# Moving recombination, PSUM order and a buffer's DMA queue around step 8 of an fp32 attention layer on one core

## The chip, the cores and the metric

The kernel runs on one core of one Trainium2 chip. The metric is device time in microseconds of one execution. The engines are TensorE (PE; its weight loads are PEld), VectorE (DVE), ScalarE (ACT), GpSimd (POOL) and SyncE (SP, which only issues DMAs here). GpSimd can issue DMAs too; its transfers go through another queue than SP's (q0 and q1 in the page's table of queues). Each engine runs its instructions in the order in which they stand in the program, and a waiting instruction holds up all behind it on that engine.

## What is computed

One layer of an encoder trunk on 512 tokens (8 rows by 64 columns) of width 2048, in float32:

```python
h = rms_norm(x, norm_pre)
q, k, v, z = split(h @ w_in, 4)                 # w_in: 2048 x 8192
o = neighbourhood_attention(q, k, v, rpb)       # 16 heads of 128, window 8 x 16, bias, softmax
y = (o * silu(z)) @ w_out                       # w_out: 2048 x 2048
x = x + rms_norm(y, norm_post)
```

## The kernel before

Every matmul is made of three: an operand is split into hi (a cast to the fp32r type, on ScalarE, line 287) and lo (source minus hi, on VectorE, line 288), and hi·hi, lo·hi and hi·lo are added up in PSUM. Splits of the stationary operand are `split_a` (lines 159, 160).

The work is a list of 512 slots `m`, each one tile of 128 by 512 of the weights. Step 0 and step 8 (`PLAIN`) multiply plainly: 32 slots each, 16 per half `n`, twelve matmuls of 512 columns per slot into four PSUM tiles `u8_n_0` to `u8_n_3` (`mm_plain`). The other steps (1 to 7 for the projections of two heads each, 9 for the last part of the output) use seven products of sums of blocks, 56 slots, in three PSUM chains X, Y and Z (`mm_seven`, `combine`); the quarters of the result come out of additions on VectorE. The last product of step 7 ends in chain Z (`u7Z0`, `u7Z1`), and `combine` takes it out with four instructions (lines 418, 419): s minus u, e minus u, for each of two. Only then can step 8's tiles `u8_0_2` and `u8_0_3` begin, because they lie in the same PSUM buffers (tags u2, u3).

The loop runs `prep(m + 2)` (loads' tile, hi, lo), then the matmuls of slot m, then what a table `beside` has at m (`at`). In that table stand the attention of heads 14 and 15 (`turn`, `split_k`, `split_q`, `scores`, ..., `split_p`, `pv`, `gated`), which runs between the slots of step 8, and the loads that follow. A scheduler turns this into the orders of the engines: the order of the code is its priority, and instructions issued through the wrappers `sync`, `dve` and `act` stay in the order of the code among themselves; others may move.

Names that matter below:

- `raw`: 4 buffers for weights just loaded (SP, lines 254 and 261). A load waits until the instruction that reads the buffer's former tile is done. raw424 to raw455 are step 8's slots 0 to 31; raw512 and on are the tiles for the sums.
- `zw`: 2 buffers. `load_z(k)` loads a block of w_out (line 133), `prep(512 + k)` adds raw(512 + k) to it on VectorE (line 269), `keep_z(k)` stores the sum to the DRAM tile `wsum` (line 136), which step 9 reads back. `sum_prep` says in which slot this is done. The next load into the buffer waits for the store. For k = 6 and 7 zw is loaded once more, with other blocks.
- `graw`: the gated heads in DRAM, written and fetched through GpSimd's queue (lines 608, 618). The buffers t0 to t7 and the pairs gr8 to gr12 take them as step 8's stationary operand (a0_0, a0_1 and so on: tile of slot k, part).
- `k14l`, `q14l`, `pt15_1l`: lo parts of attention operands of heads 14 and 15, made on VectorE, read by TensorE's score (line 525) and output (line 596) matmuls. `zm15` is head 15's gated output (line 602), whose split is a7_2, the stationary operand of slot 15.
- `WARM`: matmuls on a tile of ones at the start (line 97), before any data is there.

Of the kernel before, what the change touches and what calls it, by code (L numbers as in the profile page):

```python
# [10 lines left out]
F32 = mybir.dt.float32  # L11
F32R = mybir.dt.float32r
AF = mybir.ActivationFunctionType
ALU = mybir.AluOpType
# [11 lines left out]
SCALE = HD ** -0.5  # L26
NEG = -1.0e30
TBL = 48
WARM = 8
SHIFT = P // 2  # L30


# [9 lines left out]
NSTEP = HEADS // 2  # L42
NPASS = 7
KH = KT // 2
SLOTS = NPASS * KH
FIRST = 2 * KT
PLAIN = (0, NSTEP)
SPAN = [FIRST if step in PLAIN else SLOTS for step in range(NSTEP + 2)]
LAST = NSTEP + 1
A11, S1, A12, N2, A22, N4, N3 = range(NPASS)  # L50
B11, B12, B21, B22 = range(4)
# [17 lines left out]
def na_block(ctx: ExitStack, tc: tile.TileContext, xT, x, gpre, gpost, w, rpb, out):  # L69
    nc = tc.nc  # L70
    sync, dve, act = (InOrder(tc, e) for e in (nc.sync, nc.vector, nc.scalar))
# [23 lines left out]
    warm = px.tile([P, P], F32, tag="T", name="warm")  # L95
    for i in range(WARM):
        nc.tensor.matmul(warm, ones, ones, start=True, stop=True)
# [30 lines left out]
    Z = {}  # L128
    wsum = dp.tile([KH, P, L], F32, name="wsum")

    def load_z(k):
        Z[k] = cp.tile([P, L], F32, tag="zw", name=f"zw{k}", bufs=2)
        nc.sync.dma_start(Z[k], w[LAST, B12, k])

    def keep_z(k):
        nc.sync.dma_start(wsum[k], Z.pop(k))


    X = {}
# [72 lines left out]
    def base(step):  # L212
        return sum(SPAN[:step])

    def where(m):

        step = 0
        while m >= SPAN[step]:
            m -= SPAN[step]
            step += 1  # L220
        p, k = divmod(m, KT if step in PLAIN else KH)
        return step, LATE[p] if step == LAST else p, k

    def is_raw(m):
        step, p, _ = where(m)
        return step in PLAIN or p not in ((0, 1, 6) if step == LAST else (0, 6))
# [6 lines left out]
    def sum_prep(m):  # L233

        m -= base(NSTEP)
        at_m = {6 + 2 * k: [k] for k in range(KH)}
        for k in range(KH):
            at_m.setdefault(22 + 2 * k if k < KH - 2 else 15 + 2 * k, []).append(KH + k)
        return [N + j for j in at_m.get(m, ())]
# [25 lines left out]
    def prep(m):  # L265
        if m >= N:
            i, k = divmod(m - N, KH)
            t = T[k] if i and k < KH - 2 else Z[k]
            nc.vector.tensor_tensor(t, t, raws.pop(m), ALU.add)
            for r in at_prep.get(m, ()):  # L270
                load_raw(r)
            return
        step, p, k = where(m)
        plain = step in PLAIN
        src = raws.pop(m) if is_raw(m) else Z[k] if (step, p) == (LAST, 6) and k >= KH - 2 else T[k]
        if not plain and p in (1, 3, 4) and (step, p) != (LAST, 1):
            nc.vector.tensor_tensor(T[k], T[k], src, ALU.add)  # L277
            src = T[k]
        if m >= N - KH:
            hi, lo = (A(k, o).rearrange("p a b -> p (a b)") for o in (S1, N3))  # L280
        else:
            hi, lo = (wp.tile([P, L], F32R, tag=t, name=f"{t}{m}") for t in ("hi", "lo"))
        W[m] = (hi, lo)
        if step == 0 and p == 0:
            take_x(k, (hi, src))
        if m:
            (act if m < 4 else nc.scalar).copy(hi, src)  # L287
        nc.vector.tensor_tensor(lo, src, hi.bitcast(F32), ALU.subtract)  # L288
        if plain:
            if step == 0 and p == 1 and k >= KH:  # L290
                load_t(1, B11, k - KH)
        elif p == 4 and step < LAST:
            load_t(step, B12, k)
        elif p == 5 and step < LAST:
            nc.vector.tensor_tensor(T[k], T[k], src, ALU.add)  # L295
        elif p == 6 and (step + 1 < NSTEP or step == LAST and k < KH - 2):
            load_t(min(step + 1, LAST), B11, k)
        elif p == 0 and step == LAST:
            nc.sync.dma_start(T[k], wsum[k])
        for r in at_prep.get(m, ()):  # L300
            load_raw(r)
# [4 lines left out]
    def chain(p):  # L306
        return "XYXYZYZ"[p]
# [4 lines left out]
    def mm_plain(m):  # L312
        step, n, k = where(m)
        if k == 0:
            if n == 0:
                U[n] = [pm.tile([P, L], F32, tag=f"u{j}", name=f"u{step}_0_{j}") for j in range(4)]
            else:
                U[n] = [px.tile([P, L], F32, tag="ST"[j // 2], name=f"u{step}_1_{j}") for j in range(4)]
        hi, lo = W.pop(m)
        kk = k % KH  # L320
        a = (A(kk, A11), A(kk, N4)) if k < KH else (A(kk, A12), A(kk, A22))
        ops = [
            (a[j // 2][:, i, j % 2 * P : j % 2 * P + P], w, j, i2)
            for i2, (i, w) in enumerate(((0, hi), (1, hi), (0, lo)))
            for j in range(4)
        ]
        if k == KT - 1:
            ops.sort(key=lambda op: op[2])
        for l, r, j, i in ops:
            nc.tensor.matmul(U[n][j], l, r, start=k == 0 and i == 0, stop=k == KT - 1 and i == 2)  # L330
            if step and k == KT - 1 and i == 2:
                finish(n, j, U[n][j], small(("v", "qk")[n], f"y{n}_{j}"))
# [12 lines left out]
    def mm_seven(m):  # L345
        step, p, k = where(m)
        c = chain(p)
        if begins(step, p) and k == 0:
            b = (step + (c == "Y")) % 2
            if step == LAST and c == "X":  # L350
                U[c] = [px.tile([P, L], F32, tag="T", name=f"u{step}{c}{s}") for s in range(2)]
            else:
                U[c] = [pm.tile([P, L], F32, tag=f"u{2 * b + s}", name=f"u{step}{c}{s}") for s in range(2)]
        if m >= N - KH:

            s, kk = divmod(2 * k, KH)
            for j in (kk, kk + 1):
                products(N - KH + j, (s,))
            if kk + 2 == KH:
                finish(2, s, U["X"][s], C[LAST]["11"][:, s, :])  # L360
                final(s)
        else:
            products(m, (0, 1))
            W.pop(m)
            if k == KH - 1:
                combine(step, p)
# [19 lines left out]
    def combine(step, p):  # L386
        u = U[chain(p)]
        c = C.setdefault(step, {})
        if step == LAST:
            combine_last(c, u, p)  # L390
        elif p == 0:
            c["12"] = pair(f"s1_{step}")
            for s in range(2):
                nc.scalar.copy(c["12"][:, s, :], u[s])
        elif p == 1:
            c["21"] = pair(f"s5_{step}")
            for s in range(2):
                nc.scalar.copy(c["21"][:, s, :], u[s])
        elif p == 2:
            c["11"] = pair(f"c11_{step}")  # L400
            for s in range(2):
                nc.scalar.activation(c["11"][:, s, :], u[s], AF.Copy, scale=rc[:, s : s + 1])
        elif p == 3:
            c["22"] = pair(f"e_{step}")
            for s in range(2):
                nc.vector.tensor_tensor(c["22"][:, s, :], u[s], c["12"][:, s, :], ALU.subtract)
            nc.vector.tensor_tensor(c["21"], c["22"], c["21"], ALU.subtract)
        elif p == 4:
            for s in range(2):
                nc.vector.tensor_tensor(c["22"][:, s, :], u[s], c["22"][:, s, :], ALU.add)  # L410
        elif p == 5:
            for s in range(2):
                nc.vector.tensor_tensor(c["12"][:, s, :], u[s], c["12"][:, s, :], ALU.subtract)
            for s in range(2):
                scale_c(c["12"], s, 0)
        else:
            for s in range(2):
                nc.vector.tensor_tensor(c["21"][:, s, :], u[s], c["21"][:, s, :], ALU.subtract)
                nc.vector.tensor_tensor(c["22"][:, s, :], c["22"][:, s, :], u[s], ALU.subtract)  # L419
            for s in range(2):  # L420
                scale_c(c["21"], s, 2)
            for s in range(2):
                scale_c(c["22"], s, 2)
# [199 lines left out]
    def at(m, f, *args):  # L623
        beside.setdefault(m, []).append(lambda: f(*args))
# [124 lines left out]
        sync.dma_start(xres[t, q], x_v[16 * t : 16 * t + 16, :, q * L : (q + 1) * L])  # L749

    for k in range(KH):
        at(base(NSTEP) + 1 + 2 * k, load_z, k)
        at(base(NSTEP) + 5 + 2 * k, keep_z, k)
    for k in (KH - 2, KH - 1):

# [18 lines left out]
            load_raw(k)  # L774
    nc.scalar.preload_act_table_set("exp_and_others")
    for m in range(-AHEAD, N):
        if m + AHEAD < N - KH:
            prep(m + AHEAD)
            for j in late_prep(m + AHEAD) + sum_prep(m + AHEAD):
                prep(j)  # L780
        if 0 <= m and m + 4 < KT:
            load_x(m + 4)
        if m < 0:
            continue
        (mm_plain if where(m)[0] in PLAIN else mm_seven)(m)
        for f in beside.get(m, ()):
            f()

# [54 lines left out]
```

## Time and profile before

| what | us |
|---|---|
| median of 3 runs | 895.12 (893.77 to 897.36) |
| profiled execution | 893.32 |
| its span, first to last instruction | 891.5 |
| first real matmul starts | 4.92 |
| step 8 begins on TensorE | 702.05 |
| step 9 begins on TensorE | 802.91 |

The page gives for each engine the busy time, its share of the span and the number of instructions. The mean granted clock of TensorE is 0.998. A row of a timeline has the start in us, the duration, engine, line, operation, output<-inputs (buffer numbers left out), shapes and the count; in brackets the idle time before it on its engine and what ended that. Rows of SPq are issues of DMAs. A row of a table of windows has the stretch, its length, then busy us and started instructions of PE, PEld, DVE, ACT and POOL, the granted clock, the mean busy share of the 16 DMA engines and GB/s.

### The profile page before, as it was taken

To read this page: it belongs to the slowest core of one execution; us is meant where nothing else is said; L and a number is where in the kernel's file an instruction comes from. 1 tells how busy PE (TensorE), PEld (TensorE's weight loads), DVE (VectorE), ACT (ScalarE), POOL (GpSimd) and SP (SyncE) were. 2 spreads that over 40 slices of the span, in tenths; PEclk is the share of its full clock that TensorE was granted. 3 is DMA by queue.
4 is the path that set the end of the run, shared out by engine and by line. 5 is a ranking of instruction groups with operands and counts; after the bars stand their busy time and mean duration, and the time that the engine had idled before them with its cause. 6 is when DMAs were issued, how large, how long until landed. Compare 5 with 4: busy or idle time off the path is not lost. (4 is left out here: it accounts for less than half of the span.)

```text
span 891.5 us, 13143 instructions
## 1 busy us (share of the span) xinstructions
PE 876.9 (98%) x4176; PEld 729.5 (82%) x4176; DVE 734.3 (82%) x1370; ACT 559.4 (63%) x1091; POOL 20.9 (2%) x42
## 2 busy tenths in 40 slices
PE   9999999999999999999999999999999999999995
PEld 8888888888888888888888888888888787888874
DVE  5467979897988898889879987998799855896995
ACT  7566857585758575856675667566756755446551
POOL 0000000000000000000000000000010100000000
PEclk9999999999999999999999999999999999999999
DMA  8768357635663676376547653764487566677875
GB/s 274 228 182 255 98 172 234 204 126 181 238 190 112 215 217 188 106 232 217 168 124 234 209 175 119 243 208 154 137 267 224 169 225 213 204 234 228 254 223 170
DMA packets 91734, 174.95 MB, mean 196 GB/s; under 512 B 10512, under 2 KB 10512, under 8 KB 91664
## 3 DMA queue, kind: packets, MB, share of 16 engines
q1 hardware_dynamic: 88992, 166.24, 60.1%
q0 software_dynamic: 2240, 7.34, 2.4%
q8 instruction: 32, 0.52, 0.2%
q10 hardware_dynamic: 432, 0.53, 0.2%
q14 instruction: 38, 0.31, 0.1%
HBM read 164.11 MB, written 9.96 MB: 195 GB/s over the span
## 5 line engine op out<-in xcount | busy, mean ns | idle before, releaser
L287 ACT CAST hi<-t 128x512 fp32r<-128x512 f32 x318 | 196.0, 619 | 127.7 <-DVE lo L288 29.2
L288 DVE TENSOR_TENSOR lo<-t,hi 128x512 fp32r<-128x512 f32 x318 | 217.0, 689 | 38.3 <-ACT hi L287 36.5
L288 DVE TENSOR_TENSOR lo<-raw,hi 128x512 fp32r<-128x512 f32 x184 | 126.1, 689 | 53.3 <-ACT hi L287 40.1
L287 ACT CAST hi<-raw 128x512 fp32r<-128x512 f32 x180 | 111.5, 620 | 90.9 <-DMA raw<-in_w 21.7
L330 PE MATMUL u<-hi,a 128*128 128x512 f32 x512 | 131.7, 394 | 1.2 <-DVE e L419 1.1
L277 DVE TENSOR_TENSOR t<-t,raw 128x512 f32<-128x512 f32 x184 | 123.1, 688 | 3.5 <-DMA raw<-in_w 3.0
L330 PEld LDWEIGHTS u<-hi,a 128*128 128x128 f32 x512 | 95.5, 189 | 21.5 <-DVE e L419 1.7
L330 PE MATMUL u<-lo,a 128*128 128x512 f32 x256 | 70.8, 390 | 0.0
L330 PEld LDWEIGHTS u<-lo,a 128*128 128x128 f32 x256 | 48.1, 188 | 10.1
L295 DVE TENSOR_TENSOR t<-t,raw 128x512 f32<-128x512 f32 x56 | 37.3, 688 | 7.3 <-DMA raw<-in_w 7.3
L377 PE MATMUL u9Y<-hi,a 128*128 128x512 f32 x96 | 26.8, 394 | 1.4 <-ACT hi L287 1.3
L377 PE MATMUL u5Y<-hi,a 128*128 128x512 f32 x96 | 26.9, 397 | 0.0
L377 PE MATMUL u3Y<-hi,a 128*128 128x512 f32 x96 | 26.9, 397 | 0.0
L377 PE MATMUL u4Y<-hi,a 128*128 128x512 f32 x96 | 26.9, 397 | 0.0
L377 PE MATMUL u6Y<-hi,a 128*128 128x512 f32 x96 | 26.9, 397 | 0.0
L377 PE MATMUL u7Y<-hi,a 128*128 128x512 f32 x96 | 26.8, 396 | 0.0
L377 PE MATMUL u1Y<-hi,a 128*128 128x512 f32 x96 | 26.8, 396 | 0.0
L377 PE MATMUL u2Y<-hi,a 128*128 128x512 f32 x96 | 26.8, 396 | 0.0
L377 PEld LDWEIGHTS u9Y<-hi,a 128*128 128x128 f32 x96 | 17.7, 188 | 6.3 <-ACT hi L287 2.3
L608 POOL DMA_DIRECT2D graw<-zm x14 | 7.8, 555 | 561.4 <-DVE zm L602 561.4
L558 ACT ACTIVATE edge<-edge,col 128x192 f32<-128x192 f32 x32 | 14.5, 454 | 8.9 <-DVE col L551 8.9
L377 PEld LDWEIGHTS u4Y<-hi,a 128*128 128x128 f32 x96 | 17.4, 189 | 3.2
(447 smaller groups left out, 1935.0 us busy)
## 6 DMA issues: line engine op xcount, KB each, us to landing
raw<-in_w SPq DMA_DIRECT2D x392, 256.0 KB, 3.0
t<-in_w SPq DMA_DIRECT2D x126, 256.0 KB, 2.9
bm<-in_rpb SPq DMA_DIRECT2D x16, 384.0 KB, 4.5
x<-in_xT SPq DMA_DIRECT2D x16, 256.0 KB, 3.8
graw<-zm POOLq DMA_DIRECT2D x14, 256.0 KB, 3.5
sq<-in_x SPq DMA_DIRECT2D x6, 512.0 KB, 5.3
xres<-in_x SPq DMA_DIRECT2D x12, 256.0 KB, 4.1
zw<-in_w SPq DMA_DIRECT2D x10, 256.0 KB, 2.7
```

The source lines that it names most:

```text
L277: nc.vector.tensor_tensor(T[k], T[k], src, ALU.add)
L287: (act if m < 4 else nc.scalar).copy(hi, src)
L288: nc.vector.tensor_tensor(lo, src, hi.bitcast(F32), ALU.subtract)
L295: nc.vector.tensor_tensor(T[k], T[k], src, ALU.add)
L330: nc.tensor.matmul(U[n][j], l, r, start=k == 0 and i == 0, stop=k == KT - 1 and i == 2)
L377: nc.tensor.matmul(U[c][s], l, r, start=begins(step, p) and k == 0 and n == 0, stop=k == KH - 1 and n == 2, skip_group_check=True,)
L558: nc.scalar.activation(p, p, AF.Exp, bias=nm[:, i : i + 1], accum_out=sm[:, i : i + 1])
L608: nc.gpsimd.dma_start(graw[h], z_of[h])
```

## The change

Five edits: nine warm-up matmuls in place of eight; zw loaded and stored through GpSimd's queue, its loads of k = 2 to 7 two slots later, and each sum for k = 0 to 7 one slot later; the last slot of step 7 put in the program ahead of the prep of two slots on, with the recombination and one lo kept in order; and in step 8's first slot the twelve matmuls listed with the tiles of the free PSUM buffers first (all of tiles 0 and 1, then 2, then 3).

```diff
-WARM = 8
+WARM = 9
...
     def load_z(k):
         Z[k] = cp.tile([P, L], F32, tag="zw", name=f"zw{k}", bufs=2)
-        nc.sync.dma_start(Z[k], w[LAST, B12, k])
+        nc.gpsimd.dma_start(Z[k], w[LAST, B12, k])
 
     def keep_z(k):
-        nc.sync.dma_start(wsum[k], Z.pop(k))
+        nc.gpsimd.dma_start(wsum[k], Z.pop(k))
...
-        at_m = {6 + 2 * k: [k] for k in range(KH)}
+        at_m = {7 + 2 * k: [k] for k in range(KH)}
...
-        nc.vector.tensor_tensor(lo, src, hi.bitcast(F32), ALU.subtract)
+        (dve if m == base(NSTEP) + 1 else nc.vector).tensor_tensor(lo, src, hi.bitcast(F32), ALU.subtract)
...
         if k == KT - 1:
             ops.sort(key=lambda op: op[2])
+        elif step and n == 0 and k == 0:
+            ops.sort(key=lambda op: max(op[2], 1))
...
+            vector = dve if step + 1 == NSTEP else nc.vector
             for s in range(2):
-                nc.vector.tensor_tensor(c["21"][:, s, :], u[s], c["21"][:, s, :], ALU.subtract)
-                nc.vector.tensor_tensor(c["22"][:, s, :], c["22"][:, s, :], u[s], ALU.subtract)
+                vector.tensor_tensor(c["21"][:, s, :], u[s], c["21"][:, s, :], ALU.subtract)
+                vector.tensor_tensor(c["22"][:, s, :], c["22"][:, s, :], u[s], ALU.subtract)
...
-        at(base(NSTEP) + 1 + 2 * k, load_z, k)
+        at(base(NSTEP) + (3 if k > 1 else 1) + 2 * k, load_z, k)
...
     for m in range(-AHEAD, N):
+        if m == base(NSTEP) - 1:
+            mm_seven(m)
         if m + AHEAD < N - KH:
             prep(m + AHEAD)
...
-        (mm_plain if where(m)[0] in PLAIN else mm_seven)(m)
+        if m != base(NSTEP) - 1:
+            (mm_plain if where(m)[0] in PLAIN else mm_seven)(m)
```

What the orders of the engines show of it. VectorE at the end of step 7, before (s5_7 and e_7 are the recombination of the last product, lo425 the split for slot 1, a5_0 and a5_1 splits of a fetched head):

```order
L160 TENSOR_TENSOR a4_1_121<-t4_140,a4_1_121 128x256
L160 TENSOR_TENSOR a5_0_124<-t5_141,a5_0_124 128x256
L288 TENSOR_TENSOR lo425_7443<-raw425_7362,hi425_7442 128x512
L418 TENSOR_TENSOR s5_7_6785<-u7Z0_7094,s5_7_6785 128x512
L419 TENSOR_TENSOR e_7_7070<-e_7_7070,u7Z0_7094 128x512
L418 TENSOR_TENSOR s5_7_6785<-u7Z1_7095,s5_7_6785 128x512
L419 TENSOR_TENSOR e_7_7070<-e_7_7070,u7Z1_7095 128x512
L288 TENSOR_TENSOR lo426_7463<-raw426_7375,hi426_7462 128x512
L160 TENSOR_TENSOR a5_1_125<-t5_141,a5_1_125 128x256
```

And of the change (the lines are those of the changed kernel; the wrapper's is 65):

```order
L161 TENSOR_TENSOR a4_1_122<-t4_141,a4_1_122 128x256
L161 TENSOR_TENSOR a5_0_125<-t5_142,a5_0_125 128x256
L161 TENSOR_TENSOR a5_1_126<-t5_142,a5_1_126 128x256
L65 TENSOR_TENSOR s5_7_6786<-u7Z0_7095,s5_7_6786 128x512
L65 TENSOR_TENSOR e_7_7071<-e_7_7071,u7Z0_7095 128x512
L65 TENSOR_TENSOR s5_7_6786<-u7Z1_7096,s5_7_6786 128x512
L65 TENSOR_TENSOR e_7_7071<-e_7_7071,u7Z1_7096 128x512
L65 TENSOR_TENSOR lo425_7458<-raw425_7363,hi425_7457 128x512
L290 TENSOR_TENSOR lo426_7464<-raw426_7376,hi426_7463 128x512
```

lo425 has gone behind the four instructions, a5_1 has come ahead of them.

VectorE some 7 us later, where the first sum and the operands of head 14's scores are made, before:

```order
L288 TENSOR_TENSOR lo428_7515<-raw428_7429,hi428_7514 128x512
L269 TENSOR_TENSOR zw0_7512<-zw0_7512,raw512_7493 128x512
L288 TENSOR_TENSOR lo429_7576<-raw429_7446,hi429_7575 128x512
L486 TENSOR_TENSOR k14l_7538<-tk14_7532,k14h_7537 128x512
L480 SCALAR_TENSOR_TENSOR q14l_7547<-tq14_7541,q14h_7546 128x512
```

And of the change:

```order
L290 TENSOR_TENSOR lo428_7516<-raw428_7430,hi428_7515 128x512
L290 TENSOR_TENSOR lo429_7577<-raw429_7461,hi429_7576 128x512
L270 TENSOR_TENSOR zw0_7513<-zw0_7513,raw512_7519 128x512
L492 TENSOR_TENSOR k14l_7539<-tk14_7533,k14h_7538 128x512
L486 SCALAR_TENSOR_TENSOR q14l_7548<-tq14_7542,q14h_7547 128x512
```

zw0 stands directly ahead of k14l. On SP its raw512 stands behind raw431 in place of ahead of it. On TensorE the score matmul that reads q14l follows directly on the one that reads k14l, and two more u matmuls (one until now between those two) stand ahead of them.

VectorE at the end of head 15's attention, before:

```order
L288 TENSOR_TENSOR lo438_7929<-raw438_7831,hi438_7928 128x512
L269 TENSOR_TENSOR zw5_7924<-zw5_7924,raw517_7932 128x512
L288 TENSOR_TENSOR lo439_7960<-raw439_7873,hi439_7959 128x512
L486 TENSOR_TENSOR pt15_0l_7955<-pt15_0_7949,pt15_0h_7954 128x512
L288 TENSOR_TENSOR lo440_7992<-raw440_7900,hi440_7991 128x512
L269 TENSOR_TENSOR zw6_7987<-zw6_7987,raw518_7995 128x512
L486 TENSOR_TENSOR pt15_1l_7983<-pt15_1_7977,pt15_1h_7982 128x512
L288 TENSOR_TENSOR lo441_8030<-raw441_7935,hi441_8029 128x512
L602 SCALAR_TENSOR_TENSOR zm15_7812<-o15_8012,zm15_7812 128x512
L160 TENSOR_TENSOR a7_2_134<-zm15_7812,a7_2_134 128x2x256
```

And of the change:

```order
L290 TENSOR_TENSOR lo438_7928<-raw438_7830,hi438_7927 128x512
L290 TENSOR_TENSOR lo439_7956<-raw439_7869,hi439_7955 128x512
L492 TENSOR_TENSOR pt15_0l_7951<-pt15_0_7945,pt15_0h_7950 128x512
L270 TENSOR_TENSOR zw5_7986<-zw5_7986,raw517_7959 128x512
L290 TENSOR_TENSOR lo440_7991<-raw440_7899,hi440_7990 128x512
L492 TENSOR_TENSOR pt15_1l_7982<-pt15_1_7976,pt15_1h_7981 128x512
L290 TENSOR_TENSOR lo441_8026<-raw441_7931,hi441_8025 128x512
L270 TENSOR_TENSOR zw6_8063<-zw6_8063,raw518_8029 128x512
L608 SCALAR_TENSOR_TENSOR zm15_7808<-o15_8008,zm15_7808 128x512
L161 TENSOR_TENSOR a7_2_135<-zm15_7808,a7_2_135 128x2x256
```

zw5 is now behind pt15_0l, and zw6 behind pt15_1l and lo441, directly ahead of zm15.

SP has 18 DMAs fewer and POOL 18 more. On POOL the loads of zw0 and zw1 stand directly behind the set-up of `ident`, ahead of everything else; zw0's store and what follows stand behind the eight fetches of t0 to t7; the two fetches of gr12 stand behind zw3's store.

## The prediction

> **What bounds the kernel now.** I read the page's first part, then who waited for whom on TensorE, then the chain that ended last.
>
> ```profile
> PE 876.9 (98%) x4176; PEld 729.5 (82%) x4176; DVE 734.3 (82%) x1370; ACT 559.4 (63%) x1091; POOL 20.9 (2%) x42
> ```
>
> TensorE is busy in 98% of the span: 14.6 us of 891.5 are left. Its waits, each with its total, count and longest in us:
>
> ```profile
> PE u9Y L377 <- ACT hi L287: 1.3, 1, 1.3
> PE o L596 <- DVE pt_1l L486: 1.1, 1, 1.1
> PE u L330 <- DVE e L419: 1.1, 1, 1.1
> PE warm L97 <- DVE ones L94: 1.1, 1, 1.1
> ```
>
> Only the second and third stand where the change works (step 8, from 702 us). The first is in the end game, the fourth before any data. What remains is mostly the stretch after the last matmul, which nothing here touches. So the edits compete for about 2.2 us, 0.25% of the time. In the chain, step 8 is one unbroken run once its attention is done, and TensorE is what finishes it:
>
> ```profile
> 756.61 46.46 PE u L330 x204
> 803.07 10.88 PE u9Z L377 x48
> ```
>
> That is 0.228 us per matmul (46.46 / 204). A microsecond won or lost by TensorE ahead of 756 us therefore moves everything behind it. In the end game each raw load is issued when the split ahead of it frees a buffer, so those waits move with it too.
>
> **The ninth warm-up matmul.** Timeline of TensorE at the start (start, duration, count at the row's end):
>
> ```profile
> 1.05 3.78 PE L97 MATMUL warm<-ones 128*128 128x128 f32 x16 [1.05 <-DVE ones L94]
> 4.92 2.83 PE L330 MATMUL u<-hi,a 128*128 128x512 f32 x8
> 5.49 1.06 PE L330 MATMUL u<-hi,a 128*128 128x512 f32 x2
> 5.91 0.91 PE L330 MATMUL u<-hi,a 128*128 128x512 f32 x2
> ```
>
> Eight in the code are 16 in the trace, 0.236 us each, ending at 4.83. A ninth adds two, 0.47 us, to 5.30; the first real matmul now starts at 4.92, so it comes 0.38 later. The early real matmuls follow each other at 0.42 us (5.49, 5.91) and not at 0.228, though the granted clock reads 1.00 at the start too (the window row below). So what is displaced runs at half rate: 0.38 / 0.42 is 0.9 of a matmul, made up later at 0.228, **+0.2 us**. If the full rate came later by as much, it would be +0.4; if data are late anyway (next part), 0.
>
> [...]
>
> **The first two zw loads now open POOL's queue.** They wait for nothing, so they go out right after POOL's last set-up instruction, instead of at 32 us:
>
> ```profile
> 1.18 0.29 POOL masks.py:199 TENSOR_SCALAR_AFFINE_SELECT ident<-ident 128x128 f32<-128x128 f32 x1
> 3.00:4.00 1.00, 1.00 (x7) 1.00 (x7) 0.17 (x1) 0.00 (x0) 0.00 (x0) 1.00 1.08 407
> 6.44 0.62 ACT L65 CAST hi<-raw 128x512 fp32r<-128x512 f32 x1
> 8.50 1.98 PE L330 MATMUL u<-hi,a 128*128 128x512 f32 x8
> ```
>
> In the window 3 to 4 the DMA engines are full (share 1.08) at 407 GB/s. Two tiles of 256 KB are 0.52 MB, 1.3 us of that, so the loads that x and raw wait for can come up to 1.3 us later. The cover is ScalarE's lead: the second tile's hi ends at 7.06 and TensorE takes it at 8.50, 1.44 us. I take **0**; with the cover gone it costs up to 1.3.
>
> [...] No row of this trace has both queues full at the start.
>
> **Recombination ahead of lo425.** VectorE up to the first e, the second e, and TensorE's wait:
>
> ```profile
> 702.04 0.76 DVE L160 TENSOR_TENSOR a<-t,a 128x256 fp32r<-128x256 f32 x2
> 702.71 0.69 DVE L288 TENSOR_TENSOR lo<-raw,hi 128x512 fp32r<-128x512 f32 x1
> 703.31 0.69 DVE L418 TENSOR_TENSOR s<-u7Z,s 128x512 f32<-128x512 f32 x1
> 703.91 0.68 DVE L419 TENSOR_TENSOR e<-e,u7Z 128x512 f32<-128x512 f32 x1
> 705.10 0.68 DVE L419 TENSOR_TENSOR e<-e,u7Z 128x512 f32<-128x512 f32 x1
> 704.64 0.74 PE L330 MATMUL u<-hi,a 128*128 128x512 f32 x2 [1.07 <-DVE e L419]
> 705.45 1.12 PE L330 MATMUL u<-hi,a 128*128 128x512 f32 x4
> ```
>
> u8_0_2 waits for the first e (ends 704.59) and u8_0_3 for the second (705.78). The order rows show that lo425 (0.60, from 702.71 to 703.31) leaves the place ahead of s, but a5_1 (half a tile wide, 0.33 by the first row's pair, 702.04 to 702.71) moves in: s starts 0.27 earlier, at 703.04. TensorE then starts u8_0_2 at 704.37 and has that group done by 705.18, one more matmul by 705.41, and waits for the second e until 705.56; it had not waited there. After these matmuls it is about **0.1 us** ahead. Bounds: 0, and 1.1 if the wait went altogether, which VectorE, busy up to s, does not allow. The sorted order of TensorE's first tile changes one row here, since it stood nearly so already.
>
> **zw0 moves behind lo429, onto k14l and q14l.** VectorE, SP's issue and TensorE:
>
> ```profile
> 709.66 0.69 DVE L288 TENSOR_TENSOR lo<-raw,hi 128x512 fp32r<-128x512 f32 x1
> 708.49 0.33 SPq L254 DMA_DIRECT2D raw<-in_w  x1
> 711.16 0.69 DVE L269 TENSOR_TENSOR zw<-zw,raw 128x512 f32<-128x512 f32 x1 [0.81 <-DMA raw<-in_w]
> 714.51 0.28 PE L525 MATMUL s<-k14h,q14l 128*128 128x256 f32 x1
> 755.96 0.33 SPq L254 DMA_DIRECT2D raw<-in_w  x1
> 761.03 0.69 DVE L269 TENSOR_TENSOR zw<-zw,raw 128x512 f32<-128x512 f32 x1 [2.31 <-DMA raw<-in_w]
> ```
>
> raw512 now stands one place later in the ring of four: it needs lo428 done (709.66 + 0.69, some 0.5 earlier by the saved and moved work, 709.9). With its own landing of 2.65 us (708.49 to 711.14) it is there at 712.55. Behind it on VectorE are zw0, k14l and q14l: q14l ends 1.9 us after zw0 starts, at 714.45. TensorE reaches that score matmul at about 714.6 (714.51, less 0.1, plus one u moved ahead of it). So nothing is lost at 2.65, 0.4 at the 3.1 us that is usual, and 2.3 at the 5.05 of the slowest such load (755.96 to 761.01). Value **+0.2**, nearest to its own landing.
>
> **zw6 leaves the place ahead of pt15_1l.** SP's issues, VectorE, TensorE:
>
> ```profile
> 744.81 0.42 SPq L254 DMA_DIRECT2D raw<-in_w  x1
> 745.72 0.69 DVE L288 TENSOR_TENSOR lo<-raw,hi 128x512 fp32r<-128x512 f32 x1 [1.43 <-ACT hi L287]
> 748.84 0.69 DVE L269 TENSOR_TENSOR zw<-zw,raw 128x512 f32<-128x512 f32 x1 [2.43 <-DMA raw<-in_w]
> 750.46 0.38 SPq L254 DMA_DIRECT2D raw<-in_w  x1
> 754.04 0.69 DVE L269 TENSOR_TENSOR zw<-zw,raw 128x512 f32<-128x512 f32 x1 [2.69 <-DMA raw<-in_w]
> 754.65 0.68 DVE L486 TENSOR_TENSOR pt_1l<-pt,pt_1h 128x512 fp32r<-128x512 f32 x1
> 755.39 0.39 PE L596 MATMUL o<-pt_1l,vh 128*128 128x256 f32 x1 [1.15 <-DVE pt_1l L486]
> ```
>
> VectorE sits 2.69 us for raw518 with pt15_1l behind it, and TensorE waits for that. In the new order only zw5 and lo440 are ahead. zw5's raw517 needs lo438 done (746.41) and took 4.0 us (744.81 to 748.82): zw5 at 750.45, lo440 at 751.05, pt15_1l done by 752.35, 1.7 us before TensorE asks (754.08). The whole gap goes: 755.39 to 754.08, **-1.3 us**.
>
> What is late next: zw6 now stands ahead of zm15, the head's last product.
>
> ```profile
> 756.65 0.69 DVE L602 SCALAR_TENSOR_TENSOR zm<-o,zm 128x512 f32<-128x512 f32 x1 [0.72 <-PE o L596]
> 757.37 0.62 ACT L159 CAST a<-zm 128x512 fp32r<-128x512 f32 x1 [3.87 <-DVE zm L602]
> 756.45 2.85 PE L330 MATMUL u<-hi,a 128*128 128x512 f32 x11
> ```
>
> zm15 feeds a7_2, ScalarE casts it by 757.99, and after seven matmuls of hi440 TensorE takes it at 758.04: no slack today. With TensorE 1.3 earlier zm15 is wanted at 755.35. raw518 can go out when lo440 is done (751.75) and took 3.5 us (750.46 to 753.96): zw6 at 755.3, zm15 at 755.9, 0.55 late. Value **+0.5**; 0 if raw518 lands in 2.65, 1.05 if in 4.0.
>
> On POOL gr12's two fetches now stand behind zw3's store. ScalarE's cast of the second, and the matmuls that want it:
>
> ```profile
> 741.25 0.62 ACT L159 CAST a<-gr 128x512 fp32r<-128x512 f32 x1 [1.04 <-DMA gr<-graw]
> 747.54 2.10 PE L330 MATMUL u<-hi,a 128*128 128x512 f32 x8
> ```
>
> The cast ends 5.7 us before TensorE starts on it; zw3's store would have to wait longer than that, so 0. The remaining moves (step 0's splits, step 8 behind zm15, SP's shorter list) fall where TensorE's list above shows no wait of a microsecond: 0, and a few tenths either way if that cover were gone.
>
> **Sum.** +0.2 + 0 - 0.1 + 0.2 - 1.3 + 0.5 = -0.5 us. The profiled execution took 893.32 (span 891.5), so 892.8; it was 1.8 faster than the median of the runs shown, 895.12, and for a median I forecast **894.6 us**.
>
> **The rivals.**
> - *No new wait* (chance 0.25): raw512 and raw518 land in about 2.65 us. Then -1.3 - 0.1 + 0.2 = -1.2, 893.9. For it: raw512 did, on quiet DMA engines. Against it: 3.5 to 5 for the later ones.
> - *Late raw tiles in front of attention* (0.2), which ends slower: the zw sums still sit in VectorE's in-order queue, now ahead of q14l and zm15. With 4.0 us for both, q14l costs 1.3 and zm15 1.05: 0.2 - 0.1 + 1.3 - 1.3 + 1.05 = +1.1, 896.2. It decides from about 3.5 us for both, where the two waits reach 1.2.
> - *Starved start* (0.1): the two early loads delay x and raw by the full 1.3 us, and ScalarE's lead of 1.44 is already spent on the later first cast. +1.3 in place of +0.2: 895.7.
> - *It does not do what it says*: the tiles of PSUM are freed hardly sooner. This is in the forecast already, as 0.1 of a wait of 1.07.
>
> **How the numbers follow.** The forecast has 0.45. The sum's ends are -1.6 (no new wait, no start cost, 0.3 at the recombination) and +1.8 (late raw tiles, and half the starved start). The three runs before spread over 3.6 us, so a median of such runs is uncertain by about 0.5 more: 893.0 to 897.4, from 895.12. About 0.5% is what a measurement of this kernel can tell from no change, 4.5 us: every case above lies within it. I leave 0.03 for faster, which would need more than all of TensorE's waits here, and 0.04 for slower, a stall in a queue that I have not seen: same 0.93.
>
> **What would show it.** Right: TensorE's list has no wait on pt_1l any more; its wait on e is 0.7 to 1.0 us, with a second small one behind it; zw waits of VectorE stand ahead of q14l and zm15, and TensorE waits for q14l or for a7_2 by a few tenths. The warm-up ends at 5.3 and the first real matmul follows at once. Wrong: a wait on x or raw before 20 us; a wait for pt_1l still there; the wait on e gone altogether; an end game that gains or loses a microsecond by itself, since its loads land in 3 to 5 us.

## The result, and the profile after

| | before | changed |
|---|---|---|
| median, us | 895.17 (893.6 to 897.36, 8 runs) | 900.41 (898.31 to 902.67, 8 runs) |
| ratio, 95% interval | | 1.0057 [1.0039, 1.0075] |
| profiled execution (span) | 893.32 (891.5) | 902.52 (900.8) |
| granted clock, mean | 0.998 | 0.994 |

The change makes the kernel 5.2 us slower. The first part of the page of the changed kernel:

```profile
PE 880.9 (98%) x4178; PEld 730.6 (81%) x4178; DVE 733.5 (81%) x1370; ACT 559.8 (62%) x1091; POOL 30.7 (3%) x60
```

TensorE's idle time went from 14.6 to 19.9 us, and its busy time rose by 4.0, though there are only two matmuls more: the trace's busy time counts a matmul longer at the lower clock, and takes in waits too short to be listed (both below). Its waits in the profile of the changed kernel (total, count, longest, in us):

```profile
PE u L335 <- DVE zm L608: 4.2, 1, 4.2
PE u9Y L382 <- DVE s L445: 1.1, 1, 1.1
PE warm L97 <- DVE ones L94: 1.1, 1, 1.1
PE u9Y L382 <- ACT hi L288: 1.0, 1, 1.0
PE tz L479 <- DVE k14l L492: 0.8, 1, 0.8
PE u L335 <- DVE e L65: 0.8, 1, 0.8
...
PE tz L479 <- DVE k9l L492: 0.2, 1, 0.2
```

The wait for pt_1l is gone, as forecast. In its place stands one of 4.2 us for zm, head 15's gated output. The timeline of the changed kernel shows what leads to it: a selection of the rows of SyncE's issues (SPq), VectorE and TensorE, each row with start, duration and, in brackets, the idle time ahead of it.

```profile
750.21 0.69 DVE L290 TENSOR_TENSOR lo<-raw,hi 128x512 fp32r<-128x512 f32 x1 [1.43 <-ACT hi L288]
750.93 0.33 SPq L255 DMA_DIRECT2D raw<-in_w  x1
756.06 0.69 DVE L270 TENSOR_TENSOR zw<-zw,raw 128x512 f32<-128x512 f32 x1 [3.12 <-DMA raw<-in_w]
756.67 0.69 DVE L290 TENSOR_TENSOR lo<-raw,hi 128x512 fp32r<-128x512 f32 x1
757.16 0.42 SPq L65 DMA_DIRECT2D gpost<-in_gpost  x1
757.68 0.38 SPq L255 DMA_DIRECT2D raw<-in_w  x1
759.07 1.09 PE L335 MATMUL u<-hi,a 128*128 128x512 f32 x4
763.04 0.69 DVE L270 TENSOR_TENSOR zw<-zw,raw 128x512 f32<-128x512 f32 x1 [4.48 <-DMA raw<-in_w]
763.64 0.68 DVE L608 SCALAR_TENSOR_TENSOR zm<-o,zm 128x512 f32<-128x512 f32 x1
764.38 3.27 PE L335 MATMUL u<-hi,a 128*128 128x512 f32 x7 [4.22 <-DVE zm L608]
767.45 0.62 PE L335 MATMUL u<-lo,a 128*128 128x512 f32 x1
```

raw517 goes out when lo438 (the row at 750.21) is done and lands 5.0 us later; zw5 adds it at 756.06. Behind zw5 stands lo440, whose end frees the buffer for raw518: it goes out at 757.68 and takes 5.2 us. zw6 takes it at 763.04, and zm15 stands behind zw6. TensorE does four matmuls of half 1; the fifth writes u8_1_3, which lies in the PSUM buffer (tag T) that o15 holds until zm15 has read it. So two loads, one after the other, have come ahead of TensorE.

The wait costs more than its length. A table of windows of the changed kernel (length; busy us and instructions of PE, PEld, DVE, ACT, POOL; granted clock; share of the DMA engines; GB/s):

```profile
763.00:765.00 2.00, 0.62 (x2) 0.53 (x3) 1.29 (x2) 0.62 (x1) 0.68 (x2) 0.88 0.46 144
765.00:767.00 2.00, 2.00 (x6) 1.56 (x5) 0.69 (x1) 0.00 (x0) 0.00 (x0) 0.50 0.79 246
767.00:769.00 2.00, 2.00 (x8) 1.62 (x7) 0.18 (x1) 0.90 (x3) 0.55 (x1) 0.77 0.02 6
769.00:771.00 2.00, 2.00 (x10) 1.64 (x10) 2.00 (x4) 2.00 (x8) 0.00 (x0) 1.00 0.37 139
```

TensorE comes back at 764.38, and from 764.50 on its granted clock is 0.50 for 3.41 us. Eight matmuls, from 764.38 to the row behind 767.45 at 767.87, took 3.49 us in place of 8 x 0.228 = 1.82: **1.7 us** more.

To place the rest I read, in each run, when four matmuls start: the first of tile u1X (step 0 is done), the last that multiplies a hi part into u7Z, the first of u9Z, and the last of u9X. The first is the column u1X, the differences are the other three. All in us; "loads" is the queue of the first two zw loads, S for SyncE's and G for GpSimd's:

| run | warm-ups, loads | u1X | steps 1-7 | step 8 | step 9 | wait on zm |
|---|---|---|---|---|---|---|
| before | 8 S | 92.8 | 608.8 | 101.3 | 78.9 | 0 |
| changed | 9 G | 93.3 | 610.8 | 107.3 | 79.6 | 4.2 |
| e1 | 9 G | 93.7 | 610.1 | 107.7 | 79.7 | 4.1 |
| e2 | 9 G | 94.0 | 612.0 | 101.2 | 78.9 | 0 |
| e3 | 9 G | 93.6 | 612.3 | 101.6 | 80.4 | 0 |
| e4 | 9 S | 93.1 | 611.8 | 105.5 | 79.5 | 2.7 |
| e5 | 8 S | 92.7 | 609.1 | 101.3 | 79.5 | 0 |
| e6 | 8 S | 92.6 | 609.6 | 100.7 | 78.7 | 0 |
| e7 | 8 S | 93.0 | 609.3 | 102.7 | 79.1 | 2.7 |
| e8 | 8 S | 92.3 | 608.6 | 99.8 | 81.0 | 0 |
| e9 | 9 S | 92.1 | 609.7 | 101.5 | 79.0 | 0 |
| e10 | 8 G | 93.8 | 609.9 | 105.2 | 81.4 | 3.2 |
| e11 | 9 G | 93.8 | 610.2 | 100.7 | 79.2 | 0 |
| e12 | 8 S | 92.6 | 609.1 | 101.2 | 79.8 | 0 |
| e13 | 9 S | 93.1 | 609.0 | 105.2 | 80.9 | 2.7 |
| e14 | 9 S | 93.1 | 610.8 | 99.7 | 78.1 | 0 |
| e15 | 8 S | 92.5 | 609.2 | 99.6 | 81.3 | 0 |

The two profiled executions differ by 9.2 us: 0.5 up to u1X, 2.0 in steps 1 to 7, 6.0 in step 8 and 0.7 in step 9. Step 8's 6.0 are the wait (4.2), the low clock (1.7), k14l (0.85) and a short wait of tq (0.2), less pt_1l (1.15) and 0.24 of the wait on e: 5.6. In the medians it is 5.2 in all, since the profile of before was 1.9 under its median and that of after 2.1 over.

### The profile page after: what moved, and what is told of

The parts are those of the page before. It is cut to its first block, busy times and chain, and to the rows that moved or that the text cites. A ratio compares the mean times of both kernels' runs of the same rounds, so it can differ in the third digit from the quotient of the medians.

```text
span 900.8 us, 13161 instructions
## 1 busy us (share of the span) xinstructions
PE 880.9 (98%) x4178; PEld 730.6 (81%) x4178; DVE 733.5 (81%) x1370; ACT 559.8 (62%) x1091; POOL 30.7 (3%) x60
## 4 chain that ended last, share of the span: by engine, by line
PE 86%; DVE 5%; DMA 4%; issue 2%; ACT 2%; POOL 0%; DVEq 0%; POOLq 0%; ACTq 0%
PE u L335 18%; DMA raw<-in_w 4%; PE u3Y L382 4%; PE u6Y L382 4%; PE u2Y L382 4%; PE u7Y L382 4%; PE u5Y L382 3%; PE u1Y L382 3%; PE u4Y L382 3%; PE s L531 3%; PE u9Y L382 2%; PE u5X L382 2%; PE u3X L382 2%; PE u2X L382 2%; PE u7X L382 2%; PE u6X L382 2%
## 5 line engine op out<-in xcount | busy, mean ns | idle before, releaser
L335 PE MATMUL u<-hi,a 128*128 128x512 f32 x512 | 133.6, 397 | 5.1 <-DVE zm L608 4.2
L382 PEld LDWEIGHTS u5Y<-hi,a 128*128 128x128 f32 x96 | 17.4, 188 | 3.2
```

The costliest lines, as they stand in the source:

```text
L382: nc.tensor.matmul(U[c][s], l, r, start=begins(step, p) and k == 0 and n == 0, stop=k == KH - 1 and n == 2, skip_group_check=True,)
```

## The experiments

**First set: where is the loss?** Three edits of the changed kernel, and itself again.

e1: no edit.

> The changed kernel as it is, once more. Theory A (place: zw6's addition stands ahead of zm15 on VectorE and waits there for raw518): the wait of TensorE for zm15 comes again, 3 to 5 us, with the clock granted at 0.5 for some us behind it, and step 8 (from the last chain-Z product of step 7 to the first of step 9) takes 106 to 108 us against 101 in the kernel before. Theory C (the loss lies outside step 8, at the start and as a drift over steps 1 to 7): step 1 begins at 93.3 again, 0.5 late, and step 7's chain Z ends at 704 again; by theory A the 1.9 us that came up between are the run's own and need not come again.

902.8, with the same wait (4.1) and step 8 at 107.7.

e2: the sums of k = 6 and 7 one slot later, with their stores and the loads behind them, so that zw6 stands behind zm15 and a7_2:

```diff
-        at_m = {7 + 2 * k: [k] for k in range(KH)}
+        at_m = {7 + 2 * k + (1 if k >= 6 else 0): [k] for k in range(KH)}
...
-        at(base(NSTEP) + 5 + 2 * k, keep_z, k)
+        at(base(NSTEP) + 5 + 2 * k + (1 if k >= 6 else 0), keep_z, k)
...
-        at(base(NSTEP) + 8 + 2 * k, load_z, k)
+        at(base(NSTEP) + 8 + 2 * k + 1, load_z, k)
```

> The changed kernel with the sums of k = 6 and 7 one slot later: on VectorE zw6 stands behind a7_2 and not ahead of zm15; nothing else moves up to there. Theory A: TensorE's wait for zm15 (4.2 us) is gone, and so is the half clock behind it (1.5 to 2 us); 5 to 6 us less than the changed kernel, a ratio to the kernel before of 0.999 to 1.002. Theory B (GpSimd's queue makes the loads land late wherever they are used): raw tiles still land in 5 us, and another wait of 2 us or more comes up in step 8; ratio 1.003 to 1.006. Theory C: at most 1 us less, ratio 1.004 to 1.006.

896.03, ratio 1.0019 [1.0007, 1.0031]. Step 8 is back at 101.2.

e3: all sums one slot earlier again.

```diff
-        at_m = {7 + 2 * k: [k] for k in range(KH)}
+        at_m = {6 + 2 * k: [k] for k in range(KH)}
```

> The changed kernel with all sums one slot earlier, as before the change (zw6 ahead of pt15_1l again, zw0 ahead of lo429). Theory A: the wait for zm15 is gone, the one for pt15_1l comes back with 0.8 to 1.5 us, none for k14l; ratio 1.000 to 1.002. Theory B: ratio 1.003 to 1.006, with waits on raw tiles that land in 5 us. Theory C: ratio 1.004 to 1.006.

899.13, ratio 1.005 [1.0022, 1.0077], over six runs from 896.77 to 903.63. Step 8 is at 101.6 with the wait on pt_1l back (1.4); what the profile (899.46) loses sits at the start, in steps 1 to 7 (612.3, the longest of all) and in step 9 (80.4). So the wait on zm is gone as theory A expected, but the time is not, and theory A's 1.000 to 1.002 was missed. What the slowest runs lost was not profiled; in the two above 901 the mean granted clock is 0.995 and 0.994, against 0.996 to 0.998 in the other four.

e4: zw through SyncE's queue again, everything else as changed.

```diff
-        nc.gpsimd.dma_start(Z[k], w[LAST, B12, k])
+        nc.sync.dma_start(Z[k], w[LAST, B12, k])
...
-        nc.gpsimd.dma_start(wsum[k], Z.pop(k))
+        nc.sync.dma_start(wsum[k], Z.pop(k))
```

> The changed kernel with zw loaded and stored through SP's queue as before, sums where the change put them. Theory A: zw6 still stands ahead of zm15, so TensorE still waits there, 2 us or more, and the start loses its 0.5 less; ratio 1.002 to 1.006. Theory B: raw518 lands in 3.5 us again, the wait for zm15 is under 1 us; ratio 0.998 to 1.001.

900.47, ratio 1.0059 [1.0037, 1.0081]: nothing won in the median. The wait on zm is 2.7 in place of 4.2 here. The view of DMA from 748 to 762 us (issues, KB each, median us from issue to landing) shows raw landing later in the changed kernel:

```profile
raw<-in_w SPq DMA_DIRECT2D x7, 256.0 KB, 5.1
gpost<-in_gpost SPq DMA_DIRECT2D x4, 256.0 KB, 4.9
wsum<-zw POOLq DMA_DIRECT2D x2, 256.0 KB, 5.4
```

and e4, in the same window:

```profile
raw<-in_w SPq DMA_DIRECT2D x7, 256.0 KB, 3.6
gpost<-in_gpost SPq DMA_DIRECT2D x2, 256.0 KB, 4.4
wsum<-zw SPq DMA_DIRECT2D x2, 256.0 KB, 5.0
```

With zw's loads and stores in one queue with raw, raw lands in 3.6 us here, as it did before (median 3.3). The second queue alone does not explain the 5.1 of the changed kernel: e3, e8 and e11 carry zw through GpSimd's queue too, and in the same window their medians are 3.5, 3.3 and 3.8; e13, which also does, has a wait of 2.7 like e4's. So GpSimd's queue does not make the wait, and whether it lengthens it is not shown.

**Second set: is zw6's place alone the cause?**

e5: the kernel before, unchanged.

> The kernel before, unchanged, to see what is usual in it. Its first profile had steps 1 to 7 (first matmul of u1X to last of u7Z) in 608.8 us, step 8 up to u9Z in 101.3 and step 9 in 78.9, and first u1X at 92.8; the changed kernels had 610.1 to 612.3 for steps 1 to 7, although the order of all instructions is the same there. If that difference belongs to the change (theory C: a drift set off at the start), this look shows 608.8 again within 0.3. If it varies from one execution to the next, this look shows 610 or more, and the difference is not the change's.

894.06; steps 1 to 7 in 609.1.

e6: the kernel before with the recombination edits alone.

```diff
-        nc.vector.tensor_tensor(lo, src, hi.bitcast(F32), ALU.subtract)
+        (dve if m == base(NSTEP) + 1 else nc.vector).tensor_tensor(lo, src, hi.bitcast(F32), ALU.subtract)
...
+        elif step and n == 0 and k == 0:
+            ops.sort(key=lambda op: max(op[2], 1))
...
+            vector = dve if step + 1 == NSTEP else nc.vector
...
+        if m == base(NSTEP) - 1:
+            mm_seven(m)
...
```

> The kernel before with the recombination edits alone (last slot of step 7 ahead of the next prep, s, e and lo425 kept in order, free PSUM tiles first). The prediction has -0.1 us for them. On all theories the wait on e falls from 1.1 to about 0.8 and the rest of step 8 stays (101.3 within 0.4); time the same as before within 0.1%. If it is 2 us or more slower, theory A (zw6's place) is not the only loss in step 8.

894.43 against 895.4, ratio 0.9998 [0.9985, 1.001]. The wait on e is 0.9, in the profiles of before 0.7 to 1.1.

e7: the kernel before with zw6's sum alone one slot later.

```diff
-        at_m = {6 + 2 * k: [k] for k in range(KH)}
+        at_m = {6 + 2 * k + (1 if k == 6 else 0): [k] for k in range(KH)}
```

> The kernel before with one sum moved: zw6 one slot later, so that it stands behind pt15_1l and lo441 and directly ahead of zm15, as in the changed kernel; all loads and stores stay on SyncE's queue, warm-up and recombination as before. Theory A (that place alone costs the time): the wait for pt_1l (1.1) goes, a wait of TensorE on zm of 2.5 to 4.2 us comes, step 8 goes from 101.3 to 104 to 107, and the time is 2.5 to 5 us above before. Theory B (GpSimd's queue): no wait on zm above 1 us, time as before or 1 us under it. Theory C (start and drift): time as before.

894.76, ratio 1.0005 [0.9988, 1.0022]. The wait is there, 2.7 us, but step 8 grew by 1.4 only, which is 2.7 less the 1.15 of pt_1l, and the time not measurably. So zw6's place alone is enough for a wait, but not for the loss. The wait also has another path here:

```profile
752.38 0.68 DVE L288 TENSOR_TENSOR lo<-raw,hi 128x512 fp32r<-128x512 f32 x1
754.84 0.33 SPq L133 DMA_DIRECT2D zw<-in_w  x1
755.26 0.38 SPq L254 DMA_DIRECT2D raw<-in_w  x1
758.22 0.69 DVE L269 TENSOR_TENSOR zw<-zw,raw 128x512 f32<-128x512 f32 x1 [2.91 <-DMA raw<-in_w]
```

lo440 (752.38) frees the buffer by 753.1, but raw518 (755.26) stands on SyncE behind a load of zw that waits until a store of zw has landed (issued at 751.66, landed at 754.82). With zw in GpSimd's queue, as changed, nothing holds raw518 up in this way. Two of the ten runs took 899; what they had more was not profiled.

e8: three places mended: as e2, and zw0 ahead of lo429 again, eight warm-ups, the first two zw loads through SyncE (`kept` is a set, not shown here, of the k whose sum has been stored).

```diff
-WARM = 9
+WARM = 8
...
-        nc.gpsimd.dma_start(Z[k], w[LAST, B12, k])
+        (nc.sync if k < 2 and k not in kept else nc.gpsimd).dma_start(Z[k], w[LAST, B12, k])
...
-        at_m = {7 + 2 * k: [k] for k in range(KH)}
+        at_m = {7 + 2 * k + (1 if k >= 6 else -1 if k == 0 else 0): [k] for k in range(KH)}
```

> The changed kernel with three places mended: zw6 and zw7 one slot later (behind a7_2), zw0 one slot earlier (ahead of lo429 again), eight warm-up matmuls and the first two zw loads through SyncE. Theory A with the start as the other loss: step 8 in 100 to 101 us with no wait on pt_1l, zm or k14l, first u1X at 92.8, so 1 us under before in those stages, 894 in the median if steps 1 to 7 are as before. If theory C's drift belongs to the remaining edits, steps 1 to 7 stay 1 to 3 us longer and the median is 895 to 897.

893.16, ratio 0.9983 [0.9972, 0.9993]: faster than before, by 0.2%. Step 8 takes 99.8, with no wait on pt_1l, zm or k14l; step 9 gives 2 us of that back, with waits of 1.5 on s and 1.3 on hi in its tile u9Y.

**Third set: the warm-up, and zw5.**

e9: the kernel before with one edit.

```diff
-WARM = 8
+WARM = 9
```

> The kernel before with nine warm-up matmuls and nothing else. So far the five looks with nine warm-ups had steps 1 to 7 in 610.1 to 612.3 us and waits of TensorE for the lo part of some head's keys (k1l, k3l, k9l, k13l, 0.2 to 0.8 each); the five with eight had 608.6 to 609.6 and no such wait. The scheduler also orders the splits of slots 7 to 10 of step 0 differently for nine. Theory D (the ninth warm-up costs more than its own 0.2 to 0.5 us, in steps 1 to 7): first u1X at 93.0 to 93.7, steps 1 to 7 in 610 to 612, time 1 to 3 us (0.1 to 0.35%) above before. Rival, the prediction's term: first u1X at 93.0, steps 1 to 7 in 608.6 to 609.6, time 0.2 to 0.5 above before. Second rival: the loads on GpSimd's queue and the moved sums set the drift off; then this run is like the first rival.

895.88 against 894.49, ratio 1.0015 [1.0003, 1.0027]. The profile (893.82) has u1X at 92.1 and 609.7 for steps 1 to 7, so it does not show where the median's 1.4 us are.

e10: the changed kernel with the same edit undone.

```diff
-WARM = 9
+WARM = 8
```

> The changed kernel with eight warm-up matmuls, everything else as changed. Theory D: first u1X at 92.3 to 93.0, steps 1 to 7 back to 608.6 to 609.6 without a wait on a k lo part, step 8 still about 106 to 107 with the wait on zm of 3 to 4 us; 1 to 3 us under the changed kernel, so 897.5 to 899.5. If the drift is not the warm-up's: 900 to 901, steps 1 to 7 over 610.

901.34 (4 runs), ratio 1.0072 [1.0052, 1.0091]: not faster. The start shows why u1X is at 93.8 all the same. Its waits:

```profile
PE u L335 <- DVE zm L608: 3.2, 1, 3.2
PE tz L479 <- DVE k14l L492: 1.8, 1, 1.8
...
PE u L335 <- ACT hi L65: 1.5, 1, 1.5
```

The last is for the second weight tile of step 0, which lands late beside the two zw loads. With eight warm-ups steps 1 to 7 still take 609.9.

e11: the changed kernel with the sums of k = 1 to 5 one slot earlier; zw6 stays directly ahead of zm15.

```diff
-        at_m = {7 + 2 * k: [k] for k in range(KH)}
+        at_m = {7 + 2 * k - (1 if 1 <= k <= 5 else 0): [k] for k in range(KH)}
```

> The changed kernel with the sums of k = 1 to 5 one slot earlier again, so that zw5 stands ahead of lo439 and pt15_0l as in the kernel before, while zw6 stays directly ahead of zm15. With zw5 ahead of lo439, raw518's load no longer waits for raw517's. Theory A2 (two loads in a row, each some 5 us, stand ahead of zm15): the wait on zm falls from 4.2 to 2.7 us or less, as in the run that moved zw6 alone, step 8 from 107.3 to 103 to 105, time 897 to 899. Theory A1 (zw6's place alone): the wait stays 4 us, step 8 at 106 to 107, time 900.

896.82, ratio 1.0024 [1.0012, 1.0036]. The wait on zm is not shorter, it is gone. VectorE's timeline in e11, with SyncE's issue of raw518:

```profile
750.46 0.69 DVE L270 TENSOR_TENSOR zw<-zw,raw 128x512 f32<-128x512 f32 x1 [0.84 <-DMA raw<-in_w]
...
753.82 0.69 DVE L290 TENSOR_TENSOR lo<-raw,hi 128x512 fp32r<-128x512 f32 x1 [1.47 <-PE u L335]
754.54 0.33 SPq L255 DMA_DIRECT2D raw<-in_w  x1
...
757.68 0.69 DVE L270 TENSOR_TENSOR zw<-zw,raw 128x512 f32<-128x512 f32 x1
758.41 0.69 DVE L608 SCALAR_TENSOR_TENSOR zm<-o,zm 128x512 f32<-128x512 f32 x1
```

zw5 runs 5.6 us earlier than in the changed kernel, lo440 (753.82) is no longer held up behind it, and raw518 goes out at 754.54 in place of 757.68. It is there 3.1 us later, when zw6's turn comes. So with zw in GpSimd's queue the wait needs both moves: zw6 ahead of zm15, and zw5 so late that raw518 waits for raw517. Undoing either takes the wait away and most of the time with it (e2 1.0019, e11 1.0024, the changed kernel 1.0057). e3 undoes both and has no such wait either, but its ratio stayed at 1.005, and why is open.

**Fourth set, on one chip: the drift in steps 1 to 7, and the start.**

e12: the kernel before. e13: the changed kernel with the first two zw loads through SyncE.

```diff
-        nc.gpsimd.dma_start(Z[k], w[LAST, B12, k])
+        (nc.sync if k < 2 and k not in kept else nc.gpsimd).dma_start(Z[k], w[LAST, B12, k])
```

> The kernel before once more, on the same chip as the three that follow, since the looks so far were spread over three chips. Theory D (the ninth warm-up adds 1 to 3 us in steps 1 to 7): steps 1 to 7 in 608.6 to 609.6. Rival E (the chips differ, the kernels don't): as long as in the runs with nine warm-ups on this chip, within 0.5.

> The changed kernel with only the first two zw loads on SyncE's queue, where they stand at slot 1 and 3 of step 0. The seven looks with these loads there had the first u1X at 92.1 to 93.1, the six with them at the head of GpSimd's queue at 93.3 to 93.8 and 94.0. Theory F (the starved start, some 1.0 us): first u1X at 93.1 or before, no wait of TensorE for a hi of step 0 above 0.4, step 8 still 105 to 107 with the wait on zm, and 1 us under the changed kernel: 899 to 900. Otherwise u1X at 93.3 or later. Theory D: steps 1 to 7 in 610 or more; rival E: like the kernel before on this chip.

e12: 894.17. e13: u1X is at 93.1 with no such wait at the start, as expected; steps 1 to 7 take 609.0, and step 8 105.2. But the median is 901.34 (899.67 to 902.78, 4 runs), ratio 1.008 [1.006, 1.0099], not 899 to 900: the microsecond is seen at u1X and not in the total.

e14 and e15: e8 with nine warm-ups, and e8 again.

> The kernel with three places mended (zw6 and zw7 behind a7_2, zw0 ahead of lo429, first zw loads through SyncE), but with nine warm-up matmuls. The same with eight gave 893.16. Theory D: 894.5 to 896, steps 1 to 7 a microsecond or more longer than in the run with eight on this chip. Rival E, with the prediction's term: 893.2 to 893.7.

> The kernel with three places mended and eight warm-up matmuls once more, for a second interval: 893.2, ratio 0.997 to 0.999. Step 8 in 100 to 101 us with no wait on zm, pt_1l or k14l above 0.3. Theory D: steps 1 to 7 in 608.6 to 609.6.

e14: 893.58, ratio 0.999 [0.9978, 1.0002]. e15: 892.94, ratio 0.9986 [0.9975, 0.9997], so e8's gain is there a second time. e14's median lies where rival E had it, but its steps 1 to 7, at 610.8, where theory D had them, and TensorE's list begins with

```profile
PE tz L482 <- DVE k3l L495: 1.1, 1, 1.1
```

Such a wait for some head's k lo part, in steps 1 to 7, stands in 7 of the 9 profiles with nine warm-ups and in 1 of the 8 with eight. The chip is not it: e14 and e15 ran on the same. It is no fixed cost either: e13 has nine, and none. Set matmul beside matmul against the profile of before, 1.8 of the 2.0 us that the changed kernel loses in steps 1 to 7, and 1.9 of 2.0 in e14, lie ahead of the heads' transposes of z (tz) and score matmuls, in part in pieces too short to be listed. The scheduler puts the splits of slots 7 to 10 of step 0 elsewhere for nine warm-ups (e9 against before: between 19 and 32 us, with the same order on each engine behind that); how that reaches steps 1 to 7 stays open.

## Why the prediction was wrong, point by point

It said 894.6 (893.0 to 897.4). What happened is its second rival, late raw tiles in front of attention, at nearly five times the price.

- **zw6 now ahead of zm15, +0.5.** This is the step that failed, in its size; the wait was where it was expected. It had raw517 out when lo438 is done, 4.0 us to land, raw518 out when lo440 is done, 3.5 to land, and zm15 0.55 late. What waits is the PSUM buffer of u8_1_3, not a7_2 as I had it, but both are wanted within 0.7 us (three matmuls). TensorE ran 3.8 us behind the profile of before at this point (742.80 against 739.01 for the same slot), which has to be added to each time. raw517 went out 0.7 later than that (746.41 + 3.8 = 750.2, measured 750.93) and landed in 5.0, 1.0 more; raw518 lost another 0.3 on SyncE behind a gpost and landed in 5.2, 1.7 more. 0.55 + 0.7 + 1.0 + 0.3 + 1.7 = 4.25, measured 4.2. I knew a load of 5.05 us, used it as an end for raw512, and left it out here, where two stand in a row and their excess adds up.
- **The clock.** The sum had no term for what TensorE paid behind its wait of 4.2 us: 3.41 us at a granted clock of 0.50, 1.7 us. The waits of 2.7 us in e4 and e13 were followed by 3.4 us at 0.50 too (last section). The mean granted clock is 0.994 or 0.995 in six of the changed kernel's eight runs and 0.997 in two, so most of them seem to have paid for it.
- **gr12's fetches behind zw3's store, 0.** They went out no later for standing there (738.88 against 735.04, while TensorE was 3.8 behind), but took longer: 6.2 us for the first in place of 3.9, and 6.3 for the second in place of 5.7. ScalarE waited 1.54 us for the first, cast the second 0.7 later than before (745.74 against 741.25 + 3.8), and split the weight behind it 0.7 later. This is the 0.7 above. That zw3's store, in flight on the same queue from 737.79 to 741.44, slowed them is likely but not shown. The argument looked only at who uses gr12, not at what stands behind its cast in ScalarE's order. The row:

```profile
745.08 1.28 ACT L160 CAST a<-gr 128x512 fp32r<-128x512 f32 x2 [1.54 <-DMA gr<-graw]
```

- **pt15_1l, -1.3.** Right: the wait is gone, and e8 and e15 show it as step 8 at 99.6 to 99.8 in place of 101.2 to 101.3.
- **zw0 onto k14l, +0.2.** Right in kind, TensorE waits for k14l instead of q14l: 0.85 here, 0.6 to 1.8 in the other runs with this place, since raw512 took 3.7 us and not 2.65.
- **Recombination, -0.1.** Right as far as can be seen: the wait on e went from 1.07 to 0.83; e6 is the same as before.
- **The first two zw loads, 0.** Wrong; the rival of the starved start was right in kind, though not by its path. Six profiles with them on GpSimd's queue have u1X at 93.3 to 94.0 (mean 93.7), eleven with SyncE at 92.1 to 93.1 (mean 92.7): 1.0 us. ScalarE's second hi starts at 8.16 in the changed kernel, 6.44 before:

```profile
8.16 0.62 ACT L65 CAST hi<-raw 128x512 fp32r<-128x512 f32 x1 [0.89 <-DMA raw<-in_w]
```

  TensorE's hi matmuls of that second tile start at 8.84 to 9.52 in the six profiles, at 7.73 to 8.81 in the eleven. The first tile was not late: the first real matmul starts at 5.03 against 4.92. The delay shows only behind it. In the total the microsecond is not seen (e4 and e13, without it, are no faster than the changed kernel).
- **The ninth warm-up, +0.2.** Too small in one comparison (e9, 1.4 us, 0.3 to 2.4), 0.6 and not certain in the second (893.58 in e14 less 892.94 in e15), and of the other sign in the third (e10, with eight, is 0.9 slower than the changed kernel, not certain either). At the start it costs 0.1 at most: the first real matmul starts at 4.77 to 4.96 with eight and at 4.89 to 5.03 with nine, not 0.38 later, since with eight there were some 0.3 us to spare (the last warm-up matmul starts at 4.41, they follow each other at 0.21, and the first real one starts at 4.92). The first eight real matmuls took 2.08 to 3.12 us in the profiles with eight and 2.06 to 3.14 in those with nine, so no gain from the ninth shows in them. (The granted clock of 1.00 that the prediction read at 3 to 4 us stands for no entry: the trace's record of it begins at 6.53 in the profile of before.) Where the ninth costs, it is probably in the waits of steps 1 to 7, of which the prediction had nothing.

## What to carry to other kernels

Work that waits for a load should not stand in an in-order queue ahead of what the critical engine wants (zw6 ahead of zm15 cost a wait of 4.2 us here); and where two such loads share a ring of buffers, the second goes out only when the first has been consumed (raw518 at 757.68, behind zw5 at 756.06 and lo440), so price the chain with the slowest landing for both. A transfer moved to a second queue was not free for the first one here: with the two loads that could then start at once, ScalarE's cast of the second weight tile started at 8.16 in place of 6.44, and u1X came 1.0 us later in the mean of the profiles. A stall of TensorE can cost more than its length: the 4.2 us of the changed kernel cost 1.7 more, and of six stalls of 2.67 to 4.22 us four were followed by a lower clock and two were not.

## What was not expected of the hardware

How long an idle TensorE kept its clock did not depend on the length of the idle time alone. The six waits on zm, with the granted clock in the windows behind each; in e1, e4 and e13 the time of the fall and the length of the low stretch are worked out from the mean clock of windows of 1 and 2 us:

| run | wait, us | it ends at | granted clock behind it | it falls at |
|---|---|---|---|---|
| changed | 4.22 | 764.38 | 0.50 for 3.41 us | 764.50 |
| e1 | 4.09 | 764.40 | 0.50 for 3.4 us | 765.1 |
| e4 | 2.73 | 763.28 | 0.50 for 3.4 us | 764.8 |
| e13 | 2.67 | 760.20 | 0.50 for 3.4 us | 761.4 |
| e10 | 3.17 | 763.38 | 1.00 | |
| e7 | 2.68 | 759.57 | 1.00 | |

Windows of e13, whose wait ends at 760.2, and of e10, whose wait ends at 763.4:

```profile
760.00:762.00 2.00, 1.80 (x7) 1.39 (x8) 0.84 (x2) 0.62 (x1) 0.38 (x1) 0.86 0.84 213
762.00:764.00 2.00, 2.00 (x6) 1.58 (x5) 0.28 (x1) 0.83 (x3) 0.29 (x1) 0.50 0.27 109
```

```profile
764.00:766.00 2.00, 2.00 (x10) 1.58 (x9) 0.69 (x1) 0.46 (x1) 0.00 (x0) 1.00 0.81 253
766.00:768.00 2.00, 2.00 (x10) 1.64 (x10) 1.74 (x3) 2.00 (x9) 0.55 (x1) 1.00 0.03 8
```

The clock fell 0.1 to 1.5 us after TensorE was back at its matmuls, and e13 lost it behind 2.67 us while e7 kept it through 2.68 and e10 through 3.17. What decides is not shown by these runs.
